# Two-layer encoder trunk: values of the differential heads projected four heads at a time, 512 columns wide, on the even pairs of heads

## The chip, the cores and the metric

One core of one Trainium2 chip runs the whole program. The metric is the device time of one execution in microseconds (us). A core has a matmul engine (PE; PEld is its loading of stationary operands), a vector engine (DVE), a scalar engine (ACT), GpSimd (POOL) and an engine that here only issues transfers (SP). Each works through its own list of instructions in order; semaphores join the lists.

## The reference

Two layers, each on 512 tokens of width 1024. Branch A, which the change concerns, has 8 differential heads: two score maps per head of width 64, values of width 128.

```python
h = rmsnorm(x, g_norm)
z = jnp.einsum('bsd,dn->bsn', h, w_in)
dq, dk, dv, dg, lq, lk, lv, lg, mq, mg, mgate = jnp.split(z, splits, axis=-1)
...
s = jnp.einsum('bqmhd,bkmhd->bmhqk', qblk, k) * scale + bias
p = jax.nn.softmax(s, axis=-1)
w = p[:, 0] - lam * p[:, 1]
return jnp.einsum('bhqk,bkhe->bqhe', w, v)
...
o_a = rmsnorm(o_a) * (1.0 - lam_init)
y_a = jnp.einsum('bse,ed->bsd', o_a * silu(dg), w_br_diff)
```

Branch B is a dilated attention with four heads, each in three groups, and branch M attends to 256 memory tokens. The three are gated, merged and projected, and added to x.

## The kernel before

Every float32 operand of a large matmul is split in two float32r parts, hi and lo: ACT copies hi (`split`, L95), DVE subtracts to get lo (L96). A product is then three matmuls (`mm3`, L167 to L169): hi by hi, hi by lo, lo by hi. Weights come by `prefetch` (L148): a transfer into `w_raw` (3 buffers), then the split into `w_hi` (4 buffers) and `w_lo` (3 buffers), two tiles ahead of their use. A tile's slot is taken over by the tile that comes four (hi) or three (lo) later, once PE has read the old one for the last time.

There are two kinds of projection. `proj_fm` (L171) has the weights stationary and streams 512 tokens: 24 matmuls of 128x512 for 128 output columns. `proj_tm` (L334) has 128 tokens stationary and streams weight columns: four accumulators in PSUM (one for each block of 128 tokens, c), four weight tiles (k2) of 256 rows each, 24 matmuls for each tile; it hands control back after each tile. The accumulators come from a pool with the tag "mm", four buffers in all, and its slots are given out in the order in which the Python code asks for them.

A layer's attention goes through j = 0 to 3. In step j, `weave` (L657) runs `dil_proj` (six `proj_fm` and one `proj_tm` of 384 columns) beside `diff_att` (heads 2j and 2j+1), and then `diff_proj` for j+1 beside `dil_att` of step j. Weights in the call of `weave` say how steps of the two generators are mixed. After each j, `diff_norm` (L435) squares the two heads' outputs (`f_osb` to `f_sq`, ACT L440), splits the square in `f_sqh` and `f_sql`, sums over channels with two matmuls into `f_ms` (an "mm" buffer, PE L443 and L444), then adds epsilon on ACT (L446) and takes a reciprocal on DVE (L447). A scheduler puts the recorded instructions in an order for each engine; the weaving order is its input.

`diff_proj` (L351) makes, for two heads, four `proj_fm` (K, Q, K, Q) with their copies to `f_k`, `f_qh`, `f_ql`: of each accumulator, one half of the partitions is copied and scaled to `f_qh` (ACT L368), the same is copied again to the other half of the partitions (ACT L371), and DVE does the low parts. The scores `f_s` are two matmuls (L407 with `f_qh`, L408 with `f_ql`). Then `proj_tm` makes the values with key `dv`.

In branch B a score tile is `d_s1` (mm3, L506) and `d_s2` (L509), both from a PSUM tag "s" with two buffers that `f_s` also uses; DVE reads them at L510 and L513, ACT takes the exponential (L516). Both branches transpose their weights by PE into `wT_ps` (L384), split them (`f_wThi`, `f_wTlo`, `d_wThi`), and multiply with the values into `f_o` and `d_o`.

Of the kernel before, what the change touches and what calls it, by code (L numbers as in the profile page):

```python
# [10 lines left out]
F32R = mybir.dt.float32r  # L11
# [9 lines left out]
DQ, DK, DV, DG = 0, 1024, 2048, 3072  # L21
# [12 lines left out]


def diff_v_cols(j):
    return [(0, 256, DV + j * 256)]


def dil_v_cols(h):  # L40
    return [(g * 128, (g + 1) * 128, LV + g * 512 + h * 128) for g in range(3)]
# [3 lines left out]
def encoder_kernel(ctx: ExitStack, tc: tile.TileContext, x, mem, g_norm, w_in, diff_lambda,  # L45
                   w_mem_kv, g_mem, w_br_diff, w_br_dil, w_br_mem, w_out, rel_bias, g_final,
                   buckets, maskrows, partrows, out):
    nc = tc.nc
# [36 lines left out]
    def f32(ap):  # L85
        return ap.bitcast(F32)

    def mm(shape, name="mm"):
        return ps.tile(shape, F32, tag="mm", name=name, bufs=4)
# [4 lines left out]
    def split(hi, lo, src):  # L94
        nc.scalar.activation(hi, src, AF.Copy)  # L95
        nc.vector.tensor_tensor(out=lo, in0=src, in1=f32(hi), op=ALU.subtract)  # L96


    def weight_order():

        def fm(l, col):
            return ("in", l, col), 8, 128, [(0, 8, 0, 128, w_in[l, :, col:col + 128])]

        def tm(l, key, n, cols):
            for k2 in range(4):
                rows = w_in[l, k2 * 256:(k2 + 1) * 256]
                yield (key, l, k2), 2, n, [(0, 2, c0, c1, rows[:, col:col + c1 - c0]) for c0, c1, col in cols]

        def wide(l, key, src, c0):
            for k2 in range(4):  # L110
                yield (key, l, c0, k2), 2, 512, [(0, 2, 0, 512, src[l, k2 * 256:(k2 + 1) * 256, c0:c0 + 512])]

        def diff(l, j):
            for m in range(2):
                yield fm(l, DK + m * 512 + j * 128)
                yield fm(l, DQ + m * 512 + j * 128)
            yield from tm(l, ("dv", j), 256, diff_v_cols(j))

        for l in range(DEPTH):
            for h in range(4):  # L120
                yield ("mk", l, h), 8, 128, [(0, 8, 0, 128, w_mem_kv[l, :, h * 128:(h + 1) * 128])]
            yield from wide(l, "mv", w_mem_kv, 512)
            for h in range(4):
                yield fm(l, MQ + h * 128)
            yield from diff(l, 0)
            for j in range(4):
                for g in range(3):
                    yield fm(l, LK + g * 512 + j * 128)
                    yield fm(l, LQ + g * 512 + j * 128)
                yield from tm(l, ("lv", j), 384, dil_v_cols(j))  # L130
                if j < 3:
                    yield from diff(l, j + 1)
            for i in U_ORDER:
                yield fm(l, U_COLS[i])
            for d in range(8):
                ds_ = slice(d * 128, (d + 1) * 128)
                for b in range(3):
                    yield fm(l, MGATE + b * 1024 + d * 128)
                yield ("ba", l, d), 8, 128, [(0, 8, 0, 128, w_br_diff[l, :, ds_])]
                yield ("bm", l, d), 8, 128, [(0, 4, 0, 128, w_br_mem[l, :, ds_]),  # L140
                                             (4, 8, 0, 128, w_br_dil[l, :, ds_])]
            for n in range(2):
                yield from wide(l, "out", w_out, n * 512)
# [190 lines left out]
    def proj_tm(l, key, n, keep):  # L334

        os = [mm([128, n]) for _ in range(4)]
        for k2 in range(4):
            whi, wlo = weight(key, l, k2)
            for c in range(4):
                cs = slice(c * 128, (c + 1) * 128)  # L340
                for k in range(2):
                    kk = 2 * k2 + k
                    mm3(os[c], hT_hi[:, kk, cs], hT_lo[:, kk, cs], whi[:, k], wlo[:, k], kk == 0, kk == 7)
            if k2 < 3:
                yield
        for c in range(4):
            keep(c, os[c])
        yield


    def diff_proj(l, j, P):  # L351
        lanes = (slice(0, 64), slice(64, 128))
        Q, K = {}, {}
        for m in range(2):
            o = proj_fm(l, DK + m * 512 + j * 128)
            for s in range(2):
                a, b = lanes[s], lanes[1 - s]
                kt = P["ae"].tile([128, S], F32R, tag="fqk", name="f_k", bufs=12)
                nc.scalar.activation(kt[a], o[a], AF.Copy)
                nc.vector.tensor_tensor(out=kt[b], in0=o[a], in1=f32(kt[a]), op=ALU.subtract)  # L360
                K[s, m] = kt
            yield
            o = proj_fm(l, DQ + m * 512 + j * 128)
            for s in range(2):
                a, b = lanes[s], lanes[1 - s]
                qh = P["ae"].tile([128, S], F32R, tag="fqk", name="f_qh", bufs=12)
                ql = P["ae"].tile([128, S], F32R, tag="fqk", name="f_ql", bufs=12)
                nc.scalar.activation(qh[a], o[a], AF.Copy, scale=0.125)  # L368
                nc.vector.scalar_tensor_tensor(out=ql[a], in0=o[a], scalar=0.125, in1=f32(qh[a]),
                                               op0=ALU.mult, op1=ALU.subtract)  # L370
                nc.scalar.activation(qh[b], f32(qh[a]), AF.Copy)  # L371
                nc.vector.tensor_copy(ql[b], f32(ql[a]))
                Q[s, m] = (qh, ql)
            yield
        vhi = P["ae"].tile([128, 4, 256], F32R, tag="v4", name="f_vhi", bufs=2)
        vlo = P["ae"].tile([128, 4, 256], F32R, tag="v4", name="f_vlo", bufs=2)
        yield from proj_tm(l, ("dv", j), 256, lambda c, o: split(vhi[:, c], vlo[:, c], o))
        return Q, K, vhi, vlo

    def transposed(wT_hi, wT_lo, srcs, q0):  # L380
        n = len(srcs)
# [275 lines left out]
    def weave(*gens):  # L657

        done, res, live = [0] * len(gens), [None] * len(gens), set(range(len(gens)))
        while live:  # L660
            i = min(live, key=lambda i: ((done[i] + WEAVE[i]) / gens[i][1], i))
            try:
                next(gens[i][0])
                done[i] += 1
            except StopIteration as e:
                res[i] = e.value
                live.remove(i)
        return res
# [11 lines left out]
    for l in range(DEPTH):  # L680
        ae_c, ae = opened(f"ae{l}", "left")
        P = {"ae": ae}
# [44 lines left out]
        fp, _ = weave((fill_mem(), 9), (mem_all(), 8))  # L727
        lam, lam_init = lams[l]
        for j in range(4):
            dp, O = weave((dil_proj(l, j, P), 10), (diff_att(l, j, P, fp, lam), 8))  # L730
            if j < 3:
                fp, _ = weave((diff_proj(l, j + 1, P), 8), (dil_att(l, j, P, dp), 4))
            else:
                weave((dil_att(l, j, P, dp), 4))
            diff_norm(j, P, O)
# [89 lines left out]
```

## Time and profile before

| what | value |
|---|---|
| median of 3 runs | 1770.51 us (1770.02 to 1771.18) |
| the profiled execution's own time | 1770.44 us |
| its span in the trace | 1768.4 us |
| PE busy | 1743.8 us, 99% |
| DVE busy | 1005.5 us, 57% |
| ACT busy | 834.5 us, 47% |
| mean rate of transfers | 113 GB/s |

The span runs from the first to the last instruction of the trace; 2.0 us of the measured time lie around it. Durations of matmuls are modelled up to the end of their pipeline, so that successive matmuls overlap in the trace: what a matmul takes of the engine's time is the distance from its start to the start of the next one. Busy time of PE is the union of these stretches.

### The profile page before, as it was taken

To read this page: it belongs to the slowest core of one execution; us is meant where nothing else is said; L and a number is where in the kernel's file an instruction comes from. 1 tells how busy PE (TensorE), PEld (TensorE's weight loads), DVE (VectorE), ACT (ScalarE), POOL (GpSimd) and SP (SyncE) were. 2 spreads that over 40 slices of the span, in tenths; PEclk is the share of its full clock that TensorE was granted. 3 is DMA by queue.
4 is the path that set the end of the run, shared out by engine and by line. 5 is a ranking of instruction groups with operands and counts; after the bars stand their busy time and mean duration, and the time that the engine had idled before them with its cause. 6 is when DMAs were issued, how large, how long until landed. Compare 5 with 4: busy or idle time off the path is not lost.

```text
span 1768.4 us, 23429 instructions
## 1 busy us (share of the span) xinstructions
PE 1743.8 (99%) x9012; PEld 1496.0 (85%) x9012; DVE 1005.5 (57%) x1727; ACT 834.5 (47%) x1436; POOL 22.1 (1%) x45
## 2 busy tenths in 40 slices
PE   7999999999999999999999999999999999999998
PEld 6798889888888888888888898888988888888886
DVE  6566576666765663333465656658566747333333
ACT  6455555545555642222255555455454548322223
POOL 2200000000000000000000000000000000000000
PEclk9999999999999999999999999999999999999999
DMA  9643243332432643333572333324332336333342
GB/s 263 141 130 86 72 123 89 103 94 76 117 97 80 202 138 95 97 93 116 160 199 59 112 85 103 94 76 116 95 98 86 101 109 202 107 96 95 96 154 72
DMA packets 308847, 200.26 MB, mean 113 GB/s; under 512 B 14116, under 2 KB 283428, under 8 KB 308736
## 3 DMA queue, kind: packets, MB, share of 16 engines
q1 hardware_dynamic: 306704, 195.09, 38.3%
q0 software_dynamic: 2032, 3.68, 1.2%
q8 instruction: 71, 1.16, 0.3%
q14 instruction: 40, 0.33, 0.1%
HBM read 177.89 MB, written 20.83 MB: 112 GB/s over the span
## 4 chain that ended last, share of the span: by engine, by line
PE 97%; DMA 1%; ACT 1%; DVE 0%; issue 0%; SPq 0%; DVEq 0%; ACTq 0%
PE mm L167 27%; PE mm L169 27%; PE mm L168 27%; PE wT_ps L384 2%; PE f_s L407 2%; PE f_s L408 2%; DMA w_raw<-in_w_mem_kv 1%; PE f_o L168 1%; PE f_o L169 1%; PE f_o L167 1%; PE d_o L533 1%; PE d_s L509 1%; PE w_ps L522 0%; PE d_o L168 0%; PE d_o L169 0%; PE d_o L167 0%
## 5 line engine op out<-in xcount | busy, mean ns | idle before, releaser
L96 DVE TENSOR_TENSOR w_lo<-w_raw,w_hi 128x1024 fp32r<-128x1024 f32 (+2 forms) x296 | 335.8, 1135 | 436.1 <-PE mm L169 389.7
L95 ACT ACTIVATE w_hi<-w_raw 128x1024 fp32r<-128x1024 f32 (+2 forms) x296 | 293.3, 991 | 601.5 <-PE mm L168 296.0
L167 PE MATMUL mm<-hT_hi,w_hi 128*128 128x512 f32 x1344 | 529.9, 395 | 1.9 <-ACT hT_hi L95 1.9
L169 PE MATMUL mm<-hT_hi,w_lo 128*128 128x512 f32 x1344 | 527.3, 392 | 0.0
L168 PE MATMUL mm<-hT_lo,w_hi 128*128 128x512 f32 x1344 | 526.7, 392 | 0.0
L167 PEld LDWEIGHTS mm<-hT_hi,w_hi 128*128 128x128 f32 x1344 | 252.8, 188 | 53.2 <-ACT hT_hi L95 2.1
L169 PEld LDWEIGHTS mm<-hT_hi,w_lo 128*128 128x128 f32 x1344 | 252.9, 188 | 53.0 <-DVE w_lo L96 0.4
L168 PEld LDWEIGHTS mm<-hT_lo,w_hi 128*128 128x128 f32 x1344 | 253.0, 188 | 50.7
L169 PE MATMUL mm<-w_hi,hT_lo 128*128 128x384 f32 (+1 forms) x512 | 160.8, 315 | 0.0
L167 PE MATMUL mm<-w_hi,hT_hi 128*128 128x384 f32 (+1 forms) x512 | 160.0, 313 | 0.0
L168 PE MATMUL mm<-w_lo,hT_hi 128*128 128x384 f32 (+1 forms) x512 | 158.5, 310 | 0.0
L413 ACT ACTIVATE f_e<-f_e,f_st 128x512 f32<-128x512 f32 x128 | 91.9, 721 | 49.7 <-DVE f_st L410 49.7
L167 PE MATMUL mm<-u_hi,w_hi 128*128 128x512 f32 x256 | 101.2, 395 | 0.0
L169 PE MATMUL mm<-u_hi,w_lo 128*128 128x512 f32 x256 | 101.2, 395 | 0.0
L168 PE MATMUL mm<-u_lo,w_hi 128*128 128x512 f32 x256 | 101.1, 395 | 0.0
L167 PEld LDWEIGHTS mm<-w_hi,hT_hi 128*128 128x128 f32 x512 | 96.9, 189 | 1.0
L168 PEld LDWEIGHTS mm<-w_lo,hT_hi 128*128 128x128 f32 x512 | 96.8, 189 | 1.1
L169 PEld LDWEIGHTS mm<-w_hi,hT_lo 128*128 128x128 f32 x512 | 96.7, 189 | 0.0
L410 DVE CUSTOM_DVE_ANT_0 f_e<-f_s,f_bias 128x512 f32<-128x512 f32 x128 | 84.4, 681 | 6.8 <-PE f_s L408 6.7
L96 DVE TENSOR_TENSOR f_wTlo<-wT_ps,f_wThi 128x512 fp32r<-128x512 f32 x64 | 43.7, 683 | 31.4 <-ACT f_wThi L95 30.2
L615 DVE TENSOR_TENSOR mgate<-mm,mgate 128x512 f32<-128x512 f32 x48 | 33.0, 688 | 48.4 <-PE mm L169 48.4
L447 DVE RECIPROCAL f_sq<-f_sq 128x512 f32<-128x512 f32 x16 | 53.6, 3349 | 9.5 <-ACT f_sq L446 9.5
(203 smaller groups left out, 2403.9 us busy)
## 6 DMA issues: line engine op xcount, KB each, us to landing
w_raw<-in_w_in SPq DMA_DIRECT2D x168, 512.0 KB, 3.8
w_raw<-in_w_in SPq DMA_DIRECT2D x96, 128.0 KB, 2.4
w_raw<-in_w_mem_kv SPq DMA_DIRECT2D x16, 512.0 KB, 6.0
w_raw<-in_w_in SPq DMA_DIRECT2D x32, 256.0 KB, 2.9
u_raw<-u_d SPq DMA_DIRECT2D x32, 256.0 KB, 4.1
w_raw<-in_w_br_diff SPq DMA_DIRECT2D x16, 512.0 KB, 3.8
w_raw<-in_w_out SPq DMA_DIRECT2D x16, 512.0 KB, 3.9
f_bias<-tt_d SPq DMA_DIRECT2D x64, 112.0 KB, 4.1
```

The source lines that it names most:

```text
L95: nc.scalar.activation(hi, src, AF.Copy)
L96: nc.vector.tensor_tensor(out=lo, in0=src, in1=f32(hi), op=ALU.subtract)
L167: nc.tensor.matmul(o, lhsT=lh, rhs=rh, start=start, stop=False)
L168: nc.tensor.matmul(o, lhsT=lh, rhs=rl, start=False, stop=False)
L169: nc.tensor.matmul(o, lhsT=ll, rhs=rh, start=False, stop=stop)
L384: nc.tensor.transpose(t[:, i], s, ident)
L407: nc.tensor.matmul(sp, lhsT=qh[:, cs], rhs=K[s, m], start=True, stop=False)
L408: nc.tensor.matmul(sp, lhsT=ql[:, cs], rhs=K[s, m], start=False, stop=True)
L410: nc.vector.tensor_tensor_reduce(out=em.rearrange("p (c b) -> p c b", c=4), in0=sp, in1=bt[:, 3 - c:7 - c], op0=ALU.add, op1=ALU.min, scal ...
L413: nc.scalar.activation(em, em, AF.Exp, scale=-1.0, bias=stt[:, m:m + 1], accum_out=stt[:, 2 + m:3 + m])
L447: nc.vector.reciprocal(sq, sq)
L615: nc.vector.tensor_tensor(out=g, in0=y, in1=g, op=ALU.mult)
```

## The change

`diff_proj` for even j now projects the values of four heads at a time, 512 columns, and for odd j it makes none: it uses the second half of what j-1 left in the list `V`. A layer then has 2 instead of 4 such projections, each with four weight tiles of 512 KB instead of 256 KB. `weave` gets 8 or 4 as the weight of `diff_proj`, since the odd ones have only four steps. `f_vhi` and `f_vlo` double in size (tag "v4"), and the descriptor scratch of the transfers that POOL issues goes from its default of 16384 to 2048 bytes per partition.

```diff
 def diff_v_cols(j):
-    return [(0, 256, DV + j * 256)]
+    return [(0, 512, DV + j * 256)]
...
             for m in range(2):
                 yield fm(l, DK + m * 512 + j * 128)
                 yield fm(l, DQ + m * 512 + j * 128)
-            yield from tm(l, ("dv", j), 256, diff_v_cols(j))
+            if j % 2 == 0:
+                yield from tm(l, ("dv", j), 512, diff_v_cols(j))
...
+    V = []
+
     def diff_proj(l, j, P):
...
-        vhi = P["ae"].tile([128, 4, 256], F32R, tag="v4", name="f_vhi", bufs=2)
-        vlo = P["ae"].tile([128, 4, 256], F32R, tag="v4", name="f_vlo", bufs=2)
-        yield from proj_tm(l, ("dv", j), 256, lambda c, o: split(vhi[:, c], vlo[:, c], o))
-        return Q, K, vhi, vlo
+        if j % 2 == 0:
+            vhi, vlo = V[:] = [P["ae"].tile([128, 4, 512], F32R, tag="v4", name="f_v" + p, bufs=2) for p in ("hi", "lo")]
+            yield from proj_tm(l, ("dv", j), 512, lambda c, o: split(vhi[:, c], vlo[:, c], o))
+        half = slice(j % 2 * 256, j % 2 * 256 + 256)
+        return Q, K, V[0][:, :, half], V[1][:, :, half]
...
             if j < 3:
-                fp, _ = weave((diff_proj(l, j + 1, P), 8), (dil_att(l, j, P, dp), 4))
+                fp, _ = weave((diff_proj(l, j + 1, P), 8 if j % 2 else 4), (dil_att(l, j, P, dp), 4))
...
-    nc = bacc.Bacc("TRN2", target_bir_lowering=False, num_devices=1)
+    nc = bacc.Bacc("TRN2", target_bir_lowering=False, num_devices=1, dynamic_dma_scratch_size=2048)
```

The order of instructions moves at the places where an odd `diff_proj` ends. Names stand as output<-inputs with the number of the buffer behind each, and semaphores that a row waits for behind "waits". Line numbers of the changed kernel are up to four higher than those of before.

First place, PE where step j=0 gives way to j=1 in the first layer, before the change. The value projection's last matmul (`mm_2177`), scores of the next heads (`f_s`), the norm of the last heads (`f_ms`) and the rest of branch B (`d_o`, `w23_ps`) stand mixed:

```order
L169 MATMUL mm_2177<-w_hi_2210,hT_lo_89 128x256
L407 MATMUL f_s_2385<-f_k_1974,f_qh_2011 128x512
L408 MATMUL f_s_2385<-f_k_1974,f_ql_2012 128x512
L407 MATMUL f_s_2391<-f_k_2095,f_qh_2132 128x512
L408 MATMUL f_s_2391<-f_k_2095,f_ql_2133 128x512
L443 MATMUL f_ms_2356<-f_sqh_2351,ones_82 128x512 [waits DVE_49]
L444 MATMUL f_ms_2356<-f_sql_2352,ones_82 128x512
L167 MATMUL d_o_1914<-d_wThi_2144,d_vhi_1693 128x256 [waits Activation_49]
L407 MATMUL f_s_2444<-f_k_1974,f_qh_2011 128x512 [waits DVE_49]
L408 MATMUL f_s_2444<-f_k_1974,f_ql_2012 128x512
```

The same place after the change. Two rows ahead of the first one shown here ends the last K/Q projection, `mm_2179`, whose Q the row with `f_qh_2204` reads (the row between is the first half of `f_ms_2222`), and `mm_2280` is the first projection of the next step:

```order
L448 MATMUL f_ms_2222<-f_sql_2218,ones_82 128x512
L537 MATMUL d_o_1914<-d_w23_1917,d_v23_1695 128x128 [waits Activation_49]
L537 MATMUL d_o_1914<-d_w23_1917,d_v23_1695 128x128
L388 MATMUL wT_ps_2081<-ident_75,d_e_2068 128x128 [waits PE_49]
L388 MATMUL wT_ps_2081<-ident_75,d_e_2068 128x128 x3
L411 MATMUL f_s_2251<-f_k_1974,f_qh_2052 128x512 [waits DVE_49]
L412 MATMUL f_s_2251<-f_k_1974,f_ql_2053 128x512
L411 MATMUL f_s_2257<-f_k_2123,f_qh_2204 128x512 [waits DVE_49,Activation_49]
L411 MATMUL f_s_2310<-f_k_1974,f_qh_2052 128x512 [waits DVE_49]
L412 MATMUL f_s_2310<-f_k_1974,f_ql_2053 128x512
L447 MATMUL f_ms_2235<-f_sqh_2230,ones_82 128x512 [waits Activation_49]
L168 MATMUL mm_2280<-hT_hi_88,w_hi_2094 128x512
```

Before, the value projection's 96 matmuls stood between the end of the last K/Q projection and the first row that reads its Q; now eight rows stand there, two of `f_ms`, two of `d_o`, two of `wT_ps` (four transposes) and two of `f_s`. What ACT has in its list there after the change, in order, is this (`w_hi_2347` takes the slot of `w_hi_2023`, which `mm_2179` reads up to its last matmul but one):

```order
L95 ACTIVATE w_hi_2347<-w_raw_2345 128x1024 [waits DMAHW1_49,PE_49]
L371 ACTIVATE f_qh_2204<-mm_2179 64x512 [waits PE_49]
L444 ACTIVATE f_sq_2229<-f_osb_1826 128x512 [waits PE_49]
L450 ACTIVATE f_sq_2216<-f_ms_2222,eps_t_84 128x512 [waits PE_49]
L95 ACTIVATE d_wThi_2064<-wT_ps_2081 128x4x128 [waits PE_49]
L374 ACTIVATE f_qh_2204<-f_qh_2204 64x512 [waits Activation_49]
```

Both copies of the last Q now stand behind the weight split and around the norm's work. The same pattern stands where j=2 gives way to j=3, and in the second layer: four places.

Second place, the end of a layer's attention (j=3). PE before the change, from the first scores of the last branch-B head on:

```order
L509 MATMUL d_s2_5191<-d_k_4855,d_q_4922 128x128
L443 MATMUL f_ms_5329<-f_sqh_5324,ones_82 128x512 [waits Activation_49]
L444 MATMUL f_ms_5329<-f_sql_5325,ones_82 128x512
L167 MATMUL f_o_4862<-f_wThi_4999,f_vhi_4350 128x256 [waits Activation_49]
L168 MATMUL f_o_4862<-f_wTlo_5000,f_vhi_4350 128x256 [waits DVE_49]
```

and after the change:

```order
L513 MATMUL d_s2_4923<-d_k_4587,d_q_4654 128x128
L447 MATMUL f_ms_5061<-f_sqh_5056,ones_82 128x512 [waits Activation_49]
L448 MATMUL f_ms_5061<-f_sql_5057,ones_82 128x512
L388 MATMUL wT_ps_4806<-ident_75,f_e_4793 128x128 [waits DVE_49,PE_49]
L388 MATMUL wT_ps_4806<-ident_75,f_e_4793 128x128 x3
L168 MATMUL d_s1_4944<-d_kh_4349,d_qh_4420 128x512 [waits DVE_49]
L169 MATMUL d_s1_4944<-d_kl_4350,d_qh_4420 128x512
L170 MATMUL d_s1_4944<-d_kh_4349,d_ql_4421 128x512
L168 MATMUL f_o_4594<-f_wThi_4731,f_vhi_3127 128x256 [waits Activation_49]
L513 MATMUL d_s2_4948<-d_k_4481,d_q_4552 128x128 [waits DVE_49]
L513 MATMUL d_s2_4948<-d_k_4587,d_q_4654 128x128
L169 MATMUL f_o_4594<-f_wTlo_4732,f_vhi_3127 128x256 [waits DVE_49]
```

The last transposes of the differential head (`wT_ps_4806`) and a second tile of scores (`d_s1_4944`, `d_s2_4948`) now stand ahead of most of `f_o`. Ten rows of `f_o`, a third tile of scores (`d_s1_4988`, `d_s2_4992`), `wT_ps_4931` and `f_ms_5074` follow, and then the next projection. DVE has this list there after the change:

```order
L514 ISA d_e_4918,d_st_4917<-d_s1_4919,d_b1_4899 128x512 [waits DMAHW1_49,DMAHW0_49,PE_49]
L514 ISA d_st_4917 128x1
L451 RECIPROCAL f_sq_5055<-f_sq_5055 128x512 [waits Activation_49]
L517 ISA d_e_4918,d_st_4917<-d_s2_4923,d_b2_4904,d_st_4917 128x256 [waits DVE_49,PE_49]
L517 ISA d_st_4917 128x1
L96 TENSOR_TENSOR f_wTlo_4732<-wT_ps_4806,f_wThi_4731 128x4x128 [waits Activation_49]
L514 ISA d_e_4943,d_st_4942<-d_s1_4944,d_b1_4899 128x512 [waits PE_49]
```

The reciprocal of the norm stands ahead of the reading of `d_s2_4923`, as it did before; what is new is that PE's `d_s2_4948`, which takes that buffer over, and `f_wTlo_4732` are now asked for while it runs. ACT's list goes on with two exponentials (`d_e_4918`, `d_e_4943`), then `f_osb_4825`, `f_sq_5068`, `f_sqh_5069`.

## Rows read from the trace of the kernel before

**Rows 1.** The page, its head and its part on busy time.

```profile
span 1768.4 us, 23429 instructions
...
PE 1743.8 (99%) x9012; PEld 1496.0 (85%) x9012; DVE 1005.5 (57%) x1727; ACT 834.5 (47%) x1436; POOL 22.1 (1%) x45
```

**Rows 2.** View of waits, PE, whole span: total, times, longest, in us.

```profile
PE f_ms L443 <- ACT f_sqh L95: 2.6, 2, 1.3
...
PE mm L167 <- ACT hT_hi L95: 1.9, 1, 1.9
```

**Rows 3.** Timeline of PE, value projection of 256 columns: start, duration, fifteen steps apart.

```profile
226.28 0.28 PE L167 MATMUL mm<-w_hi,hT_hi 128*128 128x256 f32 x1
...
228.08 0.28 PE L167 MATMUL mm<-w_hi,hT_hi 128*128 128x256 f32 x1
```

**Rows 4.** Timeline of PE: projection of 384 columns (eight steps), of 512 (six steps).

```profile
520.73 0.33 PE L167 MATMUL mm<-w_hi,hT_hi 128*128 128x384 f32 x1
...
522.12 0.34 PE L169 MATMUL mm<-w_hi,hT_lo 128*128 128x384 f32 x1
...
529.54 0.39 PE L169 MATMUL mm<-hT_hi,w_lo 128*128 128x512 f32 x1
...
530.93 0.39 PE L169 MATMUL mm<-hT_hi,w_lo 128*128 128x512 f32 x1
```

**Rows 5.** Groups by line, ACT, 100 to 520 us: busy us, mean ns, then idle.

```profile
L95 ACT ACTIVATE w_hi<-w_raw 128x1024 fp32r<-128x1024 f32 x39 | 41.3, 1062 | 34.9 <-PE mm L169 23.4 <-issue 4.8 <-PE mm L168 4.2
...
L516 ACT ACTIVATE d_e<-d_e,d_st 128x768 f32<-128x768 f32 x12 | 11.2, 937 | 6.7 <-DVE d_st L513 6.6
...
L371 ACT ACTIVATE f_qh<-f_qh 64x512 fp32r<-64x512 f32 x14 | 8.8, 631 | 0.4
...
L368 ACT ACTIVATE f_qh<-mm 64x512 fp32r<-64x512 f32 x14 | 8.2, 588 | 0.3
L95 ACT ACTIVATE d_wThi<-wT_ps 128x512 fp32r<-128x512 f32 x12 | 7.2, 598 | 4.0 <-PE wT_ps L384 3.7
...
L440 ACT ACTIVATE f_sq<-f_osb 128x512 f32<-128x512 f32 x7 | 4.4, 628 | 0.0
...
L446 ACT ACTIVATE f_sq<-f_ms,eps_t 128x512 f32<-128x512 f32 x6 | 4.1, 689 | 6.1 <-PE f_ms L444 6.1
```

**Rows 6.** Timeline of PE where j=0 gives way to j=1, six matmuls.

```profile
230.28 0.28 PE L167 MATMUL d_o<-d_wThi,d_vhi 128*128 128x256 f32 x1
...
231.62 0.28 PE L169 MATMUL d_o<-d_wThi,d_vlo 128*128 128x256 f32 x1
```

**Rows 7.** Timeline of PE, ACT and DVE at the end of the first layer's attention.

```profile
524.62 0.39 PE L444 MATMUL f_ms<-f_sql,ones 128*128 128x512 f32 x1
...
525.11 0.69 ACT L446 ACTIVATE f_sq<-f_ms,eps_t 128x512 f32<-128x512 f32 x1 [0.43 <-PE f_ms L444]
...
525.22 0.68 DVE L510 CUSTOM_DVE_ANT_0 d_e<-d_s,d_b 128x512 f32<-128x512 f32 x1
...
525.83 3.35 DVE L447 RECIPROCAL f_sq<-f_sq 128x512 f32<-128x512 f32 x1
...
527.04 0.39 PE L169 MATMUL d_s<-d_kh,d_ql 128*128 128x512 f32 x1
...
528.75 0.50 PE L443 MATMUL f_ms<-f_sqh,ones 128*128 128x512 f32 x1 [1.32 <-ACT f_sqh L95]
...
529.10 0.39 DVE L513 CUSTOM_DVE_ANT_0 d_e<-d_s,d_b,d_st 128x256 f32<-128x256 f32 x1
```

**Rows 8.** Groups by line, DVE, 100 to 520 us.

```profile
L96 DVE TENSOR_TENSOR f_wTlo<-wT_ps,f_wThi 128x512 fp32r<-128x512 f32 x31 | 21.2, 683 | 15.7 <-ACT f_wThi L95 15.1
```

**Rows 9.** Windows: length, busy us (instructions) by engine, granted clock, share of DMA, GB/s.

```profile
48.50:51.90 3.40, 3.40 (x10) 2.62 (x9) 0.42 (x1) 0.00 (x0) 2.36 (x4) 0.50 0.80 146
```

**Rows 10.** The page's slices of POOL (44.2 us each); bias tiles, first and last reader.

```profile
POOL 2200000000000000000000000000000000000000
...
L410 DVE CUSTOM_DVE_ANT_0 f_e<-f_s,f_bias x128: 624/684/692, 120.7 to 1382.4; 128x512 f32<-128x512 f32 x128
```

## Prediction

> **What bounds the kernel now.** I read the page's busy times first: the matmul engine (PE) is busy for 1743.8 of the 1768.4 us of the span, the vector engine (DVE) for 57% and the scalar engine (ACT) for 47% of it [rows 1]. So the time is the sum of what PE takes for each matmul and of its waits. The view of waits then says how little PE waits: after the start there are two waits of 1.3 us for `f_ms`, at the end of each layer's attention, and one of 1.9 us at 47 us, in the start-up [rows 2]. In the timeline a matmul's duration reaches to the end of its pipeline, so I take distances between starts. The change touches PE in two ways: its matmuls become fewer and wider, and the list of PE loses filling work at the places where an odd `diff_proj` ends. The second question matters more, because with an engine that is 99% busy each new wait adds to the time in full.
>
> **Term 1, the wider matmuls.** A value projection has 4 tiles x 4 accumulators x 2 x 3 = 96 matmuls. Eight projections of 256 columns (768 matmuls) become four of 512 columns (384). The 256-column ones follow each other at (228.08 - 226.28)/15 = 0.120 us [rows 3], which is 92.2 us for 768. The trace has no 512-column matmul with the same operands, but it has the 384-column ones with the same kind of operands, at (522.12 - 520.73)/8 = 0.174 us. One straight line through 0.120 and 0.174 gives 0.228 us at 512; the 512-column matmuls of the other projection are at (530.93 - 529.54)/6 = 0.232 us [rows 4]. So 384 of them take 87.4 us by the line (nearest in kind, which I use), 89.1 us by the other. The gain is 4.8 us. Its lower bound is 3.1 us, by that row; a loss is excluded, since 0.232 is under twice 0.120.
>
> For this term the Trainium skill has a rule that speaks against it. In "TensorE: Matmul & The Clock Gate", section "Wait — 56ns, not 53.3ns?", back-to-back matmuls are said to start N/2.4 ns plus about 2.5 ns apart once the array is warm. By that, an estimate from the page, two of 256 columns take 218.3 ns against 215.8 ns for one of 512, the term would be 384 x 2.5 ns = 1.0 us, and the total below would be 3.8 us higher. The trace disagrees with it on both prices: 0.120 and 0.228 us [rows 3, 4], with a fixed part of about 0.012 us, so the measured one is used.
>
> Weight splits go from 32 of 512 elements per partition to 16 of 1024, and the copies of the values likewise; both become fewer, on engines with a third or more of their time free [rows 1]. I cost them at nothing: the projections' own matmuls cover them. The smaller descriptor scratch can only hold up POOL's transfers, those of the bias tables; POOL works in the first two slices of 44 us alone, and the first reader of a bias tile comes at 120.7 us [rows 10]. It is free up to some 30 us of delay, and beyond that every microsecond would count.
>
> **Term 2, the hand-over to an odd j (four places).** Before, the value projection lies between the last K/Q projection and the scores that read its Q. For odd j it is gone. PE then has eight rows until `f_s_2257`, which needs both copies of that Q, and the copies are in ACT's list behind a weight split that waits for the last read of `w_hi_2023`. I put t = 0 at the start of that read, PE's last matmul but one of the projection. ACT begins about 0.49 us after such a start (524.62 to 525.11 for an ACT instruction after a 512-column matmul [rows 7]). Then it does in order, by their mean durations [rows 5]: split 1.06, `f_qh` first half 0.59, `f_sq` 0.63, the epsilon 0.69, `d_wThi` 0.60, `f_qh` second half 0.63, together 4.20. PE gets its operand at t = 4.7. PE on its side needs 0.23 for each of the projection's last two matmuls, the two of `f_ms` and the two of `f_s` (1.38), and some 0.54 for `d_o` and four transposes: it stands ready at t = 1.9. The wait is 2.8 us. Behind it stand two more scores, the second `f_ms` (its `f_sqh` is ACT's next instruction, 0.63 us, while PE does three matmuls of 0.23: no new wait) and then the next projection, so nothing covers it. Before, the same hand-over loses about 0.45 us: from 230.28 to 231.62, 1.34 us, for two matmuls of 0.12, two of 0.23 and some 0.2 of short ones [rows 6]. The net is 2.35 us, four times: +9.4 us. Bounds: 1.3 us net, if the split (1.06) is over before Q's accumulator is; 2.8 us, if the old loss stays beside it.
>
> **Term 3, the end of each layer's attention (two places).** With less filler the transposes and a second score tile come before most of `f_o`. The reciprocal of the norm takes DVE from 525.83 for 3.35 us, and the reading of `d_s2` comes behind it, 529.10 to 529.49 [rows 7]. After the change the next `d_s2` needs that buffer. On the clock of before: PE ends `f_ms` at 524.85, does four transposes (0.36) and waits for the buffer of `d_s1`, which DVE leaves at 525.90, so 0.74 us; then three matmuls and one of `f_o` to 526.76, and it waits for `d_s2` until 529.54: 2.78 us. `f_wTlo` follows on DVE (0.68 [rows 8]) and is done at 530.2, PE is there at 529.88: 0.34 us. The last `f_ms` needs `f_osb`, `f_sq` and `f_sqh` (0.6 each), behind an exponential (0.94 [rows 5], with some 0.2 to read its sum) whose scores DVE reads last, at 531.4: 531.4 + 1.15 + 1.9 = 534.45, where PE is ready at 532.8: 1.65 us. Together 5.5 us. Before, this place lost 1.5 us (528.75 less 527.04 less one matmul of 0.23 [rows 7]). Net 4.0 us, twice: +8.0 us. Bounds: 1.5 us, if only the part from the exponential on is new, to 4.4 us.
>
> **Term 4, the clock.** After the 1.9 us wait in the start-up [rows 2] the trace has a stretch from 48.5 to 51.9 us with a granted clock of 0.50, the lower of the two levels, 1.2 GHz [rows 9]: 3.4 us in which PE does half the work, 1.7 us lost. The 1.3 us waits are followed by no such stretch. The new waits of 2.8 us are longer than the one that was, but they stand in full work, where that one stood in a thin start-up. The price is 1.7 us for each of six waits, 0 to 10.2 us together; I take one or two, +2.0 us, since a single case is all there is.
>
> **Sum.** -4.8 + 9.4 + 8.0 + 2.0 = +14.6 us on the profiled execution's 1770.44 us (span 1768.4 and 2.0 around it), which is within 0.1 us of the median 1770.51: **1785 us**, 0.8% slower. A measurement of this kernel can tell 0.2% (3.5 us) from no change.
>
> **Rivals.**
> *The gain without the waits (faster).* ACT gets to the second copy of Q before PE needs it. For it speaks that PE waits for no score at all before, though the same ACT work lies at three hand-overs a layer [rows 2]. Against it: there the value projection, 96 x 0.120 = 11.5 us, lay between; now it is 1.9 us of short rows against 4.2 us of ACT. Time: 1770.4 - 4.8 = 1765.6 us. It decides as long as the new waits add up to less than 1.3 us, that is 0.2 us at each of six places. Chance 0.18.
> *The waits at the low ends.* 4 x 1.3 + 2 x 1.5 - 4.8 = +3.4: 1773.8 us, just within 0.2%. It holds if the weight split is done ahead of the projection's end and the reciprocal starts earlier. For it: both are ordered by semaphores whose tiles I read from the list, not from a run. Chance 0.18; a third of this case lies a little over 0.2%.
> *The clock falls behind every wait.* Terms 1 to 3 with 10.2 us instead of 2.0, and the 512-column matmuls at 0.232: 1770.4 - 3.1 + 9.4 + 8.0 + 10.2 = 1794.9 us. For it: the one long wait in full view did it. Against it: one case. Chance 0.16.
> The forecast itself, 1777 to 1790 us, has 0.48.
>
> **How the numbers follow.** Faster by over 0.2% is the first rival with its waits under 1.3 us, 0.17. Within 0.2% are the rest of it and two thirds of the second, 0.13. Slower is the forecast, the third rival and the other third of the second, 0.70. The range goes from 1765, which leaves out about half of the first rival, to 1794, which leaves out the top half of the third: 0.17 outside. The forecast's own range is 1777 to 1790.
>
> **What would show it.** Right: the view of waits has PE's scores of `f_s` waiting for ACT's `f_qh` four times, 2 to 3 us each, PE's `d_s` waiting for DVE's `d_st` twice, near 2.8 us, and longer waits for `f_ms`; the 384 wide matmuls follow at 0.228 us; PE's idle time outside the start is 15 to 25 us instead of 3. Wrong: PE's waits in the attention stay near those of before, or the wide matmuls follow at 0.216 us, or more than that. The granted clock by windows behind each wait tells term 4. If the scratch matters, POOL waits and the first scores come later than 120 us.

## The result and the profile after

The changed kernel takes 1785.5 us (median of four executions, 1783.9 to 1786.3) against 1770.3 us before: the ratio is 1.0086, interval 1.0074 to 1.0098. It is slower by 15 us, at the place where the prediction had put it (1785). The page of the profiled execution begins:

```profile
span 1783.3 us, 22546 instructions
...
PE 1747.1 (98%) x8628; PEld 1482.6 (83%) x8628; DVE 1002.9 (56%) x1695; ACT 825.8 (46%) x1402; POOL 22.2 (1%) x45
```

The span is 14.9 us longer than in [rows 1], while PE is busy for only 3.3 us more: it waits, and it also works more slowly at times. The view of waits of PE (total, times, longest) names the places:

```profile
PE f_s L411 <- ACT f_qh L374: 8.0, 4, 2.0
PE d_s L513 <- DVE d_st L517: 5.0, 2, 2.5
...
PE wT_ps L388 <- DVE f_wTlo L96: 0.5, 2, 0.2
PE f_ms L447 <- ACT f_sqh L95: 0.3, 1, 0.3
```

The first line is the hand-over to an odd j: four waits of 2.0 us for the second copy of Q. The second is the end of each layer's attention: two waits of 2.5 us for the buffer that DVE reads behind the reciprocal. Neither stands in the view of before [rows 2]; the 1.3 us waits for `f_ms` there have shrunk to one of 0.3. In the timeline, the first hand-over looks like this (start, duration, then the row, idle time before it in brackets):

```profile
225.73 0.94 ACT L520 ACTIVATE d_e<-d_e,d_st 128x768 f32<-128x768 f32 x1 [0.88 <-DVE d_st L517]
...
225.95 0.48 PE L169 MATMUL mm<-hT_lo,w_hi 128*128 128x512 f32 x1
...
226.67 1.04 ACT L95 ACTIVATE w_hi<-w_raw 128x1024 fp32r<-128x1024 f32 x1
...
227.62 0.57 ACT L371 ACTIVATE f_qh<-mm 64x512 fp32r<-64x512 f32 x1
...
228.08 0.40 PE L412 MATMUL f_s<-f_k,f_ql 128*128 128x512 f32 x1
228.09 0.62 ACT L444 ACTIVATE f_sq<-f_osb 128x512 f32<-128x512 f32 x1
...
228.62 0.67 ACT L450 ACTIVATE f_sq<-f_ms,eps_t 128x512 f32<-128x512 f32 x1
...
229.19 0.58 ACT L95 ACTIVATE d_wThi<-wT_ps 128x512 fp32r<-128x512 f32 x1
...
229.79 0.63 ACT L374 ACTIVATE f_qh<-f_qh 64x512 fp32r<-64x512 f32 x1
...
230.47 0.73 PE L411 MATMUL f_s<-f_k,f_qh 128*128 128x512 f32 x2 [2.00 <-ACT f_qh L374]
```

The row at 225.95 is PE's last matmul but one of the K/Q projection, at which the prediction put t = 0. Behind an exponential (225.73), ACT does exactly the list of the prediction: weight split, first half of Q, `f_sq`, epsilon, `d_wThi`, second half of Q. PE has issued its last ready score at 228.08 and starts the next at 230.47, right behind the last of them. The end of the first layer's attention, same columns:

```profile
528.74 3.35 DVE L451 RECIPROCAL f_sq<-f_sq 128x512 f32<-128x512 f32 x1
...
529.68 0.28 PE L168 MATMUL f_o<-f_wThi,f_vhi 128*128 128x256 f32 x1
...
532.01 0.38 DVE L517 CUSTOM_DVE_ANT_0 d_e<-d_s,d_b,d_st 128x256 f32<-128x256 f32 x1
...
532.46 1.05 PE L513 MATMUL d_s<-d_k,d_q 128*128 128x128 f32 x4 [2.50 <-DVE d_st L517]
...
537.87 0.50 PE L447 MATMUL f_ms<-f_sqh,ones 128*128 128x512 f32 x1 [0.27 <-ACT f_sqh L95]
```

The reciprocal holds DVE from 528.74 to 532.1, the read of `d_s` ends at 532.4, and PE's next `d_s` starts at 532.46, after 2.50 us. The last wait, for `f_ms`, is only 0.27 us, where [rows 7] had 1.32. What may hide it is in the next view, windows behind the six waits (length, busy time by engine, granted clock, share of DMA, GB/s):

```profile
230.80:234.20 3.40, 3.40 (x16) 2.74 (x15) 3.34 (x3) 2.20 (x5) 0.00 (x0) 1.00 0.29 77
457.60:461.00 3.40, 3.40 (x9) 2.67 (x9) 3.31 (x4) 1.74 (x4) 0.00 (x0) 0.50 0.30 92
532.70:536.10 3.40, 3.40 (x17) 3.30 (x17) 2.73 (x9) 2.00 (x5) 0.00 (x0) 0.50 0.21 77
1106.10:1109.50 3.40, 3.40 (x10) 2.62 (x9) 3.34 (x3) 2.14 (x5) 0.00 (x0) 0.50 0.64 188
1334.80:1338.20 3.40, 3.40 (x10) 2.62 (x9) 3.29 (x4) 1.36 (x4) 0.00 (x0) 0.50 0.25 86
1409.90:1413.30 3.40, 3.40 (x15) 3.21 (x15) 2.41 (x8) 2.05 (x6) 0.00 (x0) 0.50 0.17 64
```

Behind five of the six waits the granted clock is 0.50, the lower level of 1.2 GHz, for 3.4 us each, as it was once in the start-up before [rows 9]. Only the first hand-over keeps its clock. The wide projection's matmuls, in a stretch of fifteen steps, start 0.227 us apart (timeline of PE):

```profile
117.70 0.39 PE L168 MATMUL mm<-w_hi,hT_hi 128*128 128x512 f32 x1
...
121.10 0.39 PE L168 MATMUL mm<-w_hi,hT_hi 128*128 128x512 f32 x1
```

One account from all starts of matmuls in both traces puts the difference together. I take the distance from each start to the next, and set apart idle time over 0.1 us and, in half-clock stretches after the first 30 us, the half that is lost. What is left is the work: 1741.8 us before, 1736.7 after, so -5.1 (of it the value projections 95.3 to 89.4, -5.9; the `wT_ps` transposes +1.9). The idle time goes from 8.5 to 19.6, +11.1. The clock's loss goes from 1.7 to 10.2, +8.5. Together +14.5 of the span's +14.9; the rest is a later start. Half of a stretch is a little high as its price: in the third hand-over's, 512-column matmuls start 0.43 us apart (1106.84 to 1109.40, six steps) instead of 0.23, so the eight that fit lose 1.6 us and not 1.7.

### The profile page after: what moved, and what is told of

Its sections match the earlier page's. It is cut to its first block, busy times and chain, and to the rows that moved or that the text cites. A ratio compares the mean times of both kernels' runs of the same rounds, so it can differ in the third digit from the quotient of the medians.

```text
span 1783.3 us, 22546 instructions
## 1 busy us (share of the span) xinstructions
PE 1747.1 (98%) x8628; PEld 1482.6 (83%) x8628; DVE 1002.9 (56%) x1695; ACT 825.8 (46%) x1402; POOL 22.2 (1%) x45
## 4 chain that ended last, share of the span: by engine, by line
PE 95%; ACT 2%; DMA 1%; issue 1%; DVE 1%; SPq 0%; ACTq 0%; DVEq 0%
PE mm L168 27%; PE mm L169 27%; PE mm L170 27%; PE wT_ps L388 2%; PE f_s L411 2%; PE f_s L412 2%; DMA w_raw<-in_w_mem_kv 1%; PE f_o L169 1%; PE f_o L170 1%; PE f_o L168 1%; PE d_s L513 1%; PE d_o L537 1%; ACT w_hi L95 1%; PE w_ps L526 0%; PE m_wT L575 0%
## 5 line engine op out<-in xcount | busy, mean ns | idle before, releaser
L96 DVE TENSOR_TENSOR w_lo<-w_raw,w_hi 128x1024 fp32r<-128x1024 f32 (+1 forms) x280 | 333.4, 1191 | 441.3 <-PE mm L170 368.9
L95 ACT ACTIVATE w_hi<-w_raw 128x1024 fp32r<-128x1024 f32 (+1 forms) x280 | 289.9, 1035 | 579.0 <-PE mm L169 242.1
L168 PE MATMUL mm<-w_hi,hT_hi 128*128 128x384 f32 (+1 forms) x384 | 137.4, 358 | 0.0
L169 PE MATMUL mm<-w_lo,hT_hi 128*128 128x384 f32 (+1 forms) x384 | 136.9, 357 | 0.0
L170 PE MATMUL mm<-w_hi,hT_lo 128*128 128x384 f32 (+1 forms) x384 | 136.8, 357 | 0.0
L169 PEld LDWEIGHTS mm<-w_lo,hT_hi 128*128 128x128 f32 x384 | 72.2, 188 | 5.5
L168 PEld LDWEIGHTS mm<-w_hi,hT_hi 128*128 128x128 f32 x384 | 72.2, 188 | 5.3
L170 PEld LDWEIGHTS mm<-w_hi,hT_lo 128*128 128x128 f32 x384 | 72.2, 188 | 4.9
L95 ACT ACTIVATE f_wThi<-wT_ps 128x512 fp32r<-128x512 f32 x64 | 38.1, 595 | 57.1 <-PE wT_ps L388 56.9
```

Source lines behind the costliest of these rows:

```text
L168: nc.tensor.matmul(o, lhsT=lh, rhs=rh, start=start, stop=False)
L169: nc.tensor.matmul(o, lhsT=lh, rhs=rl, start=False, stop=False)
L170: nc.tensor.matmul(o, lhsT=ll, rhs=rh, start=False, stop=stop)
```

## Experiments

Each kernel is the changed one with one edit, unless said otherwise. Times are medians; ratios are against the kernel before, run beside it, with their 95% interval. The medians of the kernel before beside them lie between 1770.3 and 1771.7 us, so a difference of under 1.5 us between two of these kernels is read only where they ran side by side. Lines and counts of waits are of one profiled execution.

**Filling work at the hand-overs.** For odd j+1, the first K projection of the next dilated head (`dil_first`, taken out of `dil_proj`) comes ahead of the norm, as a fifth step of `diff_proj`, whose weight is 5 there.

```diff
...
-                fp, _ = weave((diff_proj(l, j + 1, P), 8 if j % 2 else 4), (dil_att(l, j, P, dp), 4))
+                def more():
+                    r = yield from diff_proj(l, j + 1, P)
+                    if not (j % 2 == 0):
+                        return r, None
+                    f = dil_first(l, j + 1, P)
+                    yield
+                    return r, f
+
+                (fp, first), _ = weave((more(), 8 if j % 2 else 4 + (j % 2 == 0)), (dil_att(l, j, P, dp), 4))
```

> The changed kernel, with the first K projection of the next dilated head (24 matmuls of 128x512) placed ahead of the norm at the hand-overs to an odd j, where it fills the engine's list. Waits theory: the four waits of f_s for f_qh (2.0 us each in the trace, 2.2 from start to start) and the three half-clock stretches behind them (1.7 us each) go: 1785.5 - 8.6 - 5.1 = 1772 us, 1770 to 1775. Rival, the time lies in the wide matmuls, their larger weight tiles or the smaller scratch: nothing changes, 1784 to 1787.

1773.9 us, ratio 1.0019 (1.0010 to 1.0028): 11.6 us less than the changed kernel. The view of waits:

```profile
PE f_o L169 <- DVE f_wTlo L96: 5.8, 2, 2.9
...
PE f_s L411 <- DVE f_st L414: 1.8, 4, 0.4
```

The waits for `f_qh` are gone; 0.44 us remains four times, now for DVE's read of a score buffer. At the ends, waits behind the reciprocal remain (2.9 us, now of `f_o`), and of the half-clock stretches only the two there. So most of the loss was at the hand-overs, and width, tile size and scratch do not cost 15 us.

**Filling work at both places.** The first gate projection also comes beside the last dilated head.

```diff
...
-                weave((dil_att(l, j, P, dp), 4))
+                def early():
+                    o = proj_fm(l, U_COLS[U_ORDER[0]])
+                    yield
+                    return o
+
+                g0, _ = weave((early(), 1), (dil_att(l, j, P, dp), 4))
...
```

> As the one before, and the first gate projection is placed beside the last dilated head at the end of each layer's attention. Waits theory: the waits there (2.5 us for d_s, some 0.8 of smaller ones) and two half-clock stretches go too, 2 x (3.3 + 1.7) = 10 us less: 1762 us, 1759 to 1766, below the kernel before. Rival, the reciprocal holds up another reader in place of d_s: 1768 to 1772.

1772.4 us (1.0006 to 1.0023). My number was a miss by 10 us. The wait moved, as the rival had it, but to ACT's `f_sqh` and not to another reader behind the reciprocal:

```profile
PE f_ms L447 <- ACT f_sqh L95: 6.0, 2, 3.0
```

The wait for `d_s` is gone, and the norm's last matmul now waits 3.0 us for `f_sqh` at each end. One reason is that the filler's matmuls stand ahead of `f_o` and not behind it. Another is work that the filler brings to ACT (timeline of the first layer's end):

```profile
531.62 0.28 PE L170 MATMUL f_o<-f_wThi,f_vlo 128*128 128x256 f32 x1
...
531.81 1.28 ACT L184 ACT_TABLE_LOAD   x1
...
534.16 0.60 ACT L434 ACTIVATE f_osb<-f_o 128x512 f32<-128x512 f32 x1
```

The last `f_o` is over at 531.9, but ACT copies it only at 534.16: a table load of 1.28 us and the sigmoid of the early gate (L184, 0.60 us) stand ahead in its list, and the epsilon of the norm (0.68). In the kernel before, the first table load at a gate's line comes at 538.3, behind this place. No run has the filler's matmuls without the sigmoid, so how much each of the two reasons costs is not shown. This filler could not help: it did not lie between the late producer and its reader, and it put work ahead of the producer.

**The same fillers on the kernel before.**

> The kernel before, with the same fillers at its hand-overs and at the ends: 256-column projections, nothing else changed. Waits theory: it had small waits only (six hand-overs of about 0.45 us, two ends of 1.5 us), so 1770.3 - 2.7 - 3.0 = 1765 us, 1763 to 1769, and its distance to the wide kernel with both fillers is the pace of the value projections alone, 4 to 6 us. Rival, width brings nothing: both filled kernels within 1 us.

1772.5 us (1.0000 to 1.0017), no gain either, a miss again. The account from the starts of matmuls, as for the changed kernel, shows which half failed. The work fell by 2.4 us, near the 2.7 expected of the hand-overs, and 1.9 of it is in `f_s`. But idle time rose by 3.9, most of it at the ends, which now wait more than before:

```profile
PE f_ms L443 <- ACT f_sqh L95: 3.5, 2, 1.8
PE f_o L167 <- ACT f_wThi L95: 2.6, 2, 1.3
```

Here too ACT has the early gate's load and sigmoid in its list: a load at 529.60 ahead of `f_wThi`, and a second one at 532.58 ahead of the next exponential and `f_osb`, 1.28 us each. So this pair does not price the width.

**Useless matmuls in the wait.** Ten matmuls with ready operands stand ahead of the late score, overwritten afterwards.

```diff
+                        if j % 2 and s == 0 and c == 0 and m == 1:
+                            kk, qq = K[0, 0], Q[0, 0][0]
+                            for i in range(10):
+                                nc.tensor.matmul(sp, lhsT=qq[:, cs], rhs=kk, start=True, stop=True)
```

> The changed kernel, with ten matmuls of no use (operands that are ready, into the score's own accumulator, which is then overwritten) ahead of the score that waits for f_qh, 2.3 us of work in each of the four waits. Nothing is released earlier. If the half-clock stretches come from these waits, three of them go and the time falls by 5.1 us, 1779 to 1782 us. If they come from something else, or cost nothing, it stays at 1785 to 1786.

1785.6 us (1.0067 to 1.0098), the same as the changed kernel, so by its time this speaks against the theory. The trace says why it doesn't decide. Windows around the second hand-over, and two at the first layer's end:

```profile
455.00:465.00 10.00, 10.00 (x46) 8.22 (x45) 8.81 (x13) 5.98 (x11) 0.00 (x0) 1.00 0.39 107
532.70:536.10 3.40, 3.09 (x14) 3.10 (x15) 1.64 (x5) 1.03 (x2) 0.00 (x0) 0.50 0.21 77
539.50:542.90 3.40, 3.40 (x9) 2.68 (x9) 0.02 (x1) 0.00 (x0) 0.00 (x0) 0.50 0.02 5
```

No hand-over has a half-clock stretch any more (the clock of the other three windows is 1.00 too): the three of the changed kernel are gone though the score came no earlier. But the scheduler also ordered the layer's end anew, and there the waits and the stretches became more, two stretches in each layer instead of one:

```profile
PE f_ms L451 <- ACT f_sqh L95: 3.8, 2, 1.9
PE d_s L517 <- DVE d_st L521: 3.4, 2, 1.7
...
PE f_o L168 <- ACT f_wThi L95: 1.4, 2, 0.7
PE d_s L168 <- DVE d_st L518: 1.0, 2, 0.5
```

These are 9.6 us of waits at the ends against 5.8 without the edit. The rows fit the theory that the stretches behind the hand-overs come from the waits, but one execution does not show it, since such a stretch can also stay away behind a wait of the same length (next run). What bears it out is a look at all thirteen traces: from 100 us to the last matmuls they have 19 half-clock stretches, and each begins in a wait of PE of 1.5 us or more, or in the matmuls just behind one. What the stretches cost is not shown by this run's time.

**A copy in place of the reciprocal** in step j=3 (the output's factor is left uninverted there).

```diff
-            nc.vector.reciprocal(sq, sq)
+            (nc.vector.tensor_copy if j == 3 else nc.vector.reciprocal)(sq, sq)
```

> The changed kernel, with the reciprocal of the norm in step j=3 replaced by a copy (so that factor of the output is left uninverted there); the lists keep their order. Reciprocal theory: DVE frees the score buffer some 2.6 us earlier, both 2.5 us waits of d_s go, with them the half-clock stretches behind them, and part comes back as a wait for f_ms (1 to 1.5 us each): 1785.6 - 5.3 - 3.4 + 2.5 = 1779.4, 1777 to 1782 us. Rival, d_s waits for its scores' exponential or for another reader: within 1 us of 1785.6.

1777.3 us (1.0030 to 1.0061), 8.2 us less. The lists did not keep their order throughout, but PE's did at both ends (the scheduler moved rows ahead of the second and behind both). There the 2.5 us waits for `d_s` are gone and 1.3 us for `f_ms` has come back, as expected:

```profile
PE f_s L411 <- ACT f_qh L374: 8.0, 4, 2.0
...
PE f_ms L447 <- ACT f_sqh L95: 2.6, 2, 1.3
```

The reciprocal is shown to be the cause of the wait for `d_s`. The four hand-over waits are unchanged at 2.0 us, but this time only one of them has a half-clock stretch behind it (windows behind the first and the second; the clock behind the other two is 1.00):

```profile
231.00:234.40 3.40, 3.40 (x15) 2.78 (x16) 3.34 (x3) 2.51 (x5) 0.00 (x0) 1.00 0.31 77
457.80:461.20 3.40, 3.40 (x9) 2.61 (x9) 3.31 (x4) 2.00 (x5) 0.00 (x0) 0.50 0.26 73
```

The time is within the expected range partly by chance: of the 8.8 us between the two profiled executions idle time makes 2.2 and four stretches fewer 6.8 (the rest is 0.2 the other way), and two of the four are at hand-overs that the edit did not touch. The four executions of this one kernel differ in the same way: 1776.2 and 1776.7 us at a mean clock of 0.997, 1777.9 at 0.996 and 1781.0 at 0.994.

**Queries before keys** in the odd steps, so that the last projection leaves ACT one copy, not two.

```diff
...
-        for m in range(2):
-            o = proj_fm(l, DK + m * 512 + j * 128)
...
+        for m in range(2):
+            for part in ((queries, keys) if j % 2 else (keys, queries)):
+                part(m)
+                yield
```

> The changed kernel, with queries before keys in the odd steps, so that the last projection's copies are one on ACT and one on DVE instead of two on ACT. Theory: the 2.0 us waits of f_s for f_qh go, and ACT's next instruction for PE, f_sqh of the norm, now ends last, about 0.6 us earlier than the old copy did plus its own 0.6: a wait for f_ms of 1.0 to 1.5 us takes its place, and the half-clock stretches behind the hand-overs become fewer. 1785.6 - 4 x 0.8 - (0 to 5.1) = 1777 to 1783 us. Rival, nothing takes its place: 1785.6 - 8.6 - 5.1 = 1772.

1781.4 us (1.0047 to 1.0075), 4.2 us less. The reader waits 1.6 instead of 2.0 us, now for DVE's half of K and not, as I had it, for `f_sqh`; the end was ordered anew and waits differently:

```profile
PE f_s L416 <- DVE f_k L363: 6.3, 4, 1.6
PE d_s L168 <- DVE d_st L519: 3.9, 2, 2.0
PE w_ps L531 <- DVE d_wTlo L96: 2.9, 2, 1.5
```

The time fits the expected range, the instruction that takes the place does not.

**The old weaving weight of 8 for every `diff_proj`.**

```diff
-(diff_proj(l, j + 1, P), 8 if j % 2 else 4)
+(diff_proj(l, j + 1, P), 8)
```

> The changed kernel, with the old weaving weight of 8 for every diff_proj, so that its four steps come earlier against the dilated head. Theory: what is missing is filling work behind an odd diff_proj, and another weight only puts other rows where none covers them; waits of d_s and f_ms for DVE and ACT take the place of those of f_s, 1776 to 1790 us. Rival, the new weight of 4 makes the waits: 1766 to 1772.

1776.5 us (1.0021 to 1.0044), 9 us less. My range held and my reason did not: with the weight of 8 no wait over 0.1 us is left at any hand-over, though the odd steps have no value projection there either. The four K/Q steps stand in the first half of the mix again, as they did when four value steps followed them; so the last Q is projected earlier, and `d_o` and dilated scores stand between it and its readers. What is left is at the ends:

```profile
PE d_s L168 <- DVE d_st L514: 3.7, 2, 1.9
...
PE f_ms L447 <- ACT f_sqh L95: 1.5, 1, 1.5
PE w_ps L526 <- DVE d_wTlo L96: 1.5, 1, 1.5
```

and a half-clock stretch behind the second end that lasts 13.6 us, with further waits in it (PE 11.38 busy):

```profile
1395.70:1409.30 13.60, 11.38 (x34) 9.10 (x35) 2.67 (x5) 3.65 (x7) 0.00 (x0) 0.50 0.05 19
```

**The scratch alone**, on the kernel before: `dynamic_dma_scratch_size=2048`.

> The kernel before, with nothing but the descriptor scratch at 2048 instead of 16384. Theory: POOL's transfers end in the first 88 us and the first bias tile is read at 120.7 us, so no change: 1769 to 1772 us. Rival, the smaller scratch holds POOL up by more than 30 us and the scores wait: above 1774.

1771.5 us (0.9996 to 1.0015): no change that can be told, and its waits for `f_ms` are 2.6 us, two times, as in [rows 2].

**A second filler at the ends**, behind the last dilated head and ahead of the norm, on the wide kernel and on the kernel before.

```diff
...
                 g0, _ = weave((early(), 1), (dil_att(l, j, P, dp), 4))
+                g1 = proj_fm(l, U_COLS[U_ORDER[1]])
             diff_norm(j, P, O)
...
```

> The wide kernel with both fillers, and the second gate projection as well placed ahead of the norm at the end of each layer's attention, since the trace of the kernel with both fillers still waits there 3.0 us for the norm's f_sqh. Theory: these two waits and the one half-clock stretch behind them go, 6.0 + 1.7 us: 1772.4 - 7.7 = 1764.7, 1762 to 1768 us, faster than the kernel before by 0.3%. Rival, the wait only moves behind the next instruction that needs ACT: 1769 to 1773.

> The same on the kernel before: 256-column projections with all fillers. Its waits at the ends of the attention are 3.1 us each with one filler: 1772.5 - 6.2 = 1766.3, 1764 to 1769 us if they go. If the width is worth its 5.9 us of matmul pace, it stays 2 to 5 us above the wide kernel with the same fillers; if not, the two are equal.

The wide one takes 1767.4 us (0.9973 to 0.9991), faster than the kernel before by 3.0 us; the narrow one 1772.0 us (1.0004 to 1.0022). The wide one's remaining waits, then the narrow one's:

```profile
PE d_s L168 <- DVE d_st L520: 2.5, 2, 1.2
PE f_s L411 <- DVE f_st L414: 1.8, 4, 0.4
```

```profile
PE w_ps L528 <- DVE d_wTlo L96: 3.1, 2, 1.6
PE f_ms L443 <- ACT f_sqh L95: 2.3, 2, 1.2
```

The wide one was expected 2.7 us lower: 1.25 us of waits at each end remained. The narrow one was a miss of 5.7 us: its fillers stand mostly ahead of `f_o`, a gate's table load (536.77, 1.28 us) stands between `f_osb` and `f_sq` in ACT's list, and 2.7 us of waits are left at each end, each with a half-clock stretch. The two are 4.6 us apart, but waits (10.6 and 11.0 us) and clock (1.7 and 3.4) make some 2 us of that. The value projections are 95.0 and 89.3 us, 5.7 apart, but PE's other rows take 2.9 us more in the wide kernel, `f_s` 1.5 of it. So this pair shows some 3 us for the width, with lists that differ at other places too.

**Weight 8, and the fillers at the ends alone.**

> The changed kernel with the old weight of 8 and, at the end of the attention alone, two gate projections ahead of the norm. The trace with weight 8 has no wait over 0.1 us at the hand-overs, and at the ends 1.9 us for d_s, 1.5 us for w_ps or f_ms, and half-clock stretches (9 us lost in its profiled execution). Theory: the fillers take the wait of d_s, the one for f_ms (f_osb, f_sq and f_sqh behind the last f_o, 1.9 us, less four transposes) stays at 1.3 to 1.9 us in each layer, a stretch behind some: 1776.5 - 3.7 - 4 to 8 = 1765 to 1769 us. If the waits only change place, 1772 to 1777.

1767.4 us, ratio 0.9976 (0.9966 to 0.9985), 4.3 us faster than the kernel before beside it. Its one wait in the attention:

```profile
PE f_ms L447 <- ACT f_sqh L95: 3.8, 2, 1.9
```

The account from the starts of matmuls says where the gain is: the work is 6.8 us less than in the kernel before, 5.7 of it the value projections, while idle time is 1.4 and the clock's loss 1.7 more. So the wide projection pays once the new waits at the hand-overs are avoided, and of the ways tried the smallest is to leave the weight as it was and fill the ends. What the end fillers alone would do to the kernel before was not run.

## Why the prediction was right

*What bounds the kernel.* Right: the loss is PE's, in waits and in its clock, and the wider matmuls' gain is inside it.

*Term 1, -4.8 us.* Right: 0.227 us a matmul in the trace after, against 0.228 from the line through 256 and 384 columns. The sum of the starts fell by 5.9: the averages are 0.124 and 0.233, since the first matmul behind other work takes longer, and such places are 62 before (3.7 us in all) and 29 after (1.6 us). By the rule of the Trainium skill ("TensorE: Matmul & The Clock Gate", "Wait — 56ns, not 53.3ns?") the gain would have been 1.0 us, an estimate from the page's figure; the trace after disagrees with that, at 0.227 us, as the one of before did.

*Term 2, +9.4 us.* Place, mechanism and count were right: four waits, `f_s` for ACT's second copy of Q, behind the list as written down. The wait was 2.0 us idle, 2.2 from start to start, against 2.8 reckoned. Three prices were off, at the first hand-over with t = 0 at 225.95. ACT began its split at t = 0.72 and not 0.49, as it had an exponential and the reading of its sum to end first. Its six instructions took 3.75 us from 226.67 to 230.42 and not 4.20: in the timeline four of the five behind the split start about 0.1 us before the one ahead ends (228.09 + 0.62 is 228.71, the next starts at 228.62), so mean durations must not be added. Together PE got its operand at 4.5 and not 4.7. And PE stood ready at 2.36 and not 1.9: the trace has four `d_o` matmuls among the short rows where the list was read as two, and a first 512-column matmul behind short ones takes 0.32 us to the next start (227.76 to 228.08), not 0.23. What the prediction left open is why the reader stands there: it named the missing value projection; the run with weight 8 shows that the new weight of 4 has to be there too.

*Term 3, +8.0 us.* Too high. Its first part came out: the wait for `d_s` was 2.50 us idle, 2.66 from start to start, against 2.78, and the run with a copy shows the reciprocal as its cause. The rest did not. The wait of `f_o` for `f_wTlo` (0.34) is not there, and the later one for `f_ms`, put at 1.65, was 0.27 at the first end and under 0.1 at the second. A half-clock stretch lies ahead of it (532.7 to 536.1), in which PE lost some 1.7 us and ACT did not; that this hid the wait is argued and not tested. At full clock, in the run with the copy, it was 1.31, but there the wait for `d_s` is missing too. In all, idle time at the two ends rose from 2.6 to 5.8 us, by 3.2, near the low bound of 2 x 1.5.

*Term 4, +2.0 us.* Too low, and the term furthest off: I took one or two half-clock stretches behind six waits, and there were five, 8.5 us. Terms 2 and 3 together were 17.4 us and came out at about 11 of idle time and 2 of slower short rows (the transposes). These errors, +6.5 and -4.4, cancel in part; term 1 and the other rows, each 1.1 us below what was reckoned, take the rest. So the slowdown and its places were foreseen, but the total is right within 1 us by luck. My range for term 4 (0 to 10.2) and the bounds of term 2 (1.3 to 2.8) held both.

*Rivals.* The gain without the waits fell with the first trace. The low ends fell too. That the clock falls behind every wait was nearly true, at five of six. The scratch costs nothing, as the run with it alone shows.

## What to carry to other kernels

On an engine that is 99% busy, taking work away is worth its time only where the work covered nothing: before removing a block, read in the lists which late producer it hid, and put other independent work between that producer and its reader, not merely near it. Look at what the filler brings to the producer's engine, too. An instruction in order behind a weight split or a 3.35 us reciprocal is late by all that stands ahead of it, even where its engine is busy for only about half of the time. Allow for a wait of PE of some 2 us to cost up to nearly twice its length: a stretch at half clock followed four of the eight hand-over waits of 2.0 us here (three in one kernel, one in the other).

## What the runs showed of the hardware

The half-clock stretches do not follow from a wait's length alone. The same wait of 2.0 us was followed by one at three of four hand-overs in the changed kernel and at one of four in the kernel with the copy; waits of 3.0 us at both ends of the kernel with both fillers, by one of two. Of the 19 between 100 us and the last matmuls, 17 lasted 3.4 us, one 6.8 (queries before keys, from 1400.5) and one 13.6. Where useless matmuls filled the wait, none followed in the one execution profiled. One kernel's executions differed by up to 5 us with the mean clock: 1776.2 to 1781.0 us at 0.997 to 0.994.

Matmuls with 128 rows of moving float32r data started 0.120, 0.174 and 0.227 us apart at 256, 384 and 512 columns: on one line, with a fixed part of about 0.013 us each. A reciprocal of 128x512 float32 took DVE 3.35 us, the copy in its place 0.43.
